# Order of the epilogues, pace of the sparse sums and the last chunks of a PEER block

## The chip, the cores and the metric

One Trainium2 chip, of which the kernel uses one core. The metric is the device time of one execution in microseconds; the median of three runs is given. The profile is of one further execution.

## What is computed

A transformer-like block on 512 tokens of width 1024: a mixer (gated convolution and a linear recurrence), then a PEER layer, which picks 16 of 16384 single-neuron experts for each of 8 heads and each token, and a final RMS norm. The part that the change touches is the last lines of this:

```
def peer block(xb):                      # 128 tokens
    idx = the 16 best experts of each of 8 heads; g = softmax of their scores
    act = gelu(einsum('phkd,pd->phk', expert_u[idx], xb))
    coef = g * act
    return einsum('phk,phkd->pd', coef, expert_v[idx])

x = x + g2[:, None, :] * peer(h, ...)
return rmsnorm(x, final_g)               # x * rsqrt(mean(x*x) + EPS) * final_g
```

## The kernel before

The four tiles of 128 tokens are treated in two ways. **Tile 0 is sparse**: for each of its 128 (head, pick) pairs GpSimd (POOL) gathers 128 rows of `expert_u` (512 KB, L802), DVE multiplies them with the tokens and adds up each row (`dots`, L823), and later the same with rows of `expert_v`: DVE adds the gathered rows, times their coefficient, to `ys` (`sums`, L837 and L839). The dots of 64 tokens of tile 1 are made in this way too. **Tiles 1 to 3 are dense**: all 16384 experts are evaluated, in 128 chunks of 128 experts, first with `u` (U stage, `u_chunk`), then with `v` (V stage). Matrix products are made exact enough by splitting an operand in a high and a low part and doing three products (high x high, high x low, low x high).

In the V stage, chunk n's 128 x 1024 block of `expert_v` is loaded on SP's queue into one of 4 `wraw` buffers (L70), ACT rounds it to `whi` (L75), DVE subtracts to get `wlo` (L80); each has 4 buffers. For every second chunk the gated coefficients of two chunks are made: `cf` (ACT L952, DVE L954), `ch` (ACT L958) and `cl` (DVE L965). PE then does 18 products of 512 columns for a chunk: 3 for each of 3 tiles and 2 halves, into six PSUM accumulators `acc` that stay open over all 128 chunks (`v_chunk`, L1070). The last VT = 3 chunks are held back and multiplied tile by tile (`v_half`, L1061 to L1063), so that tile 1's accumulators close before those of tiles 2 and 3.

Order: from the U stage to the end of the loop over chunks the program order of each engine is the order in which the code is written (`manual_schedule`, L1001 to L1116). Each chunk's turn in the loop (L1087) issues the load for the chunk five ahead, the rounding for three ahead, the subtraction for two ahead, the coefficients, PE's products, and then some steps of the sparse generator (dots, then sums). How many is a pace: `share` (L1111) grows linearly with n over NE - VE - QV chunks, less 0.31 for each chunk after RB = 32. Gathers run up to 6 steps ahead of the sums, in 5 `rows` buffers and 2 of `rows2`.

Behind the loop stand the loads of three rows into `gt` (the gate g2, its bias, the final gain; L1081), their sum (L1083), the loads of the residual `x1d` into `wraw` buffers (L1124), and `final(t)` for tiles 1, 2, 3 and 0: multiply by the gate row, add the residual, square and add up on ACT (L1134), 1/sqrt with one Newton step (`rsqrt_small`, L106), scale, store. From L1116 on a scheduler of the language decides the order of each engine, and it interleaves the four epilogues.

Of the kernel before, what the change touches and what calls it, by code (L numbers as in the profile page):

```python
# [8 lines left out]
F32 = mybir.dt.float32  # L9
# [4 lines left out]
AF = mybir.ActivationFunctionType  # L14
OP = mybir.AluOpType
# [3 lines left out]
D = 1024  # L19
KB = 8  # L20
NT = 4
NE = 128
EPS = 1e-6
# [11 lines left out]
def block_kernel(ctx, tc, xT, small, w_ada1, w_ada, b_ada, w_in, w_r, w_i, w_out, w_q, keys, uT, u, v, final_g, out):  # L35
    nc = tc.nc
# [69 lines left out]
    def rsqrt_small(dst, src, scale, n, seed=False):  # L106
        m = const.tile([128, 64], F32, name="rs_m")[:, :n]
        t = const.tile([128, 64], F32, name="rs_t")[:, :n]
        nc.vector.tensor_scalar(m, src, scale, EPS, op0=OP.mult, op1=OP.add)
        if seed:  # L110
            nc.scalar.activation(dst, m, AF.Abs_reciprocal_sqrt)
        else:
            nc.scalar.activation(t, m, AF.Sqrt)
            nc.vector.reciprocal(dst, t)
        nc.vector.tensor_mul(t, dst, dst)
        nc.vector.tensor_mul(t, t, m)
        nc.vector.tensor_scalar(t, t, -0.5, 1.5, op0=OP.mult, op1=OP.add)
        nc.vector.tensor_mul(dst, dst, t)
# [144 lines left out]
    g2d = dram.tile([2, 512], F32, name="g2d")  # L263
# [75 lines left out]
    for cb in range(4):  # L339
# [20 lines left out]
        r = mt("r")  # L360
# [24 lines left out]
        y = mix.tile([128, T], F32, name="y", bufs=2)  # L385
# [13 lines left out]
        y = mix.tile([128, T], F32, name="y", bufs=2)  # L399
# [19 lines left out]
    x1d = dram.tile([T, D], F32, name="x1d")  # L419
# [122 lines left out]
    rowp = ctx.enter_context(tc.tile_pool(name="rowp", bufs=1))  # L542
# [243 lines left out]
    rows = {}  # L786
# [69 lines left out]
    def w_load(k):  # L856
        if k < len(jobs):
            kind, i = jobs[k]
            wraw[k] = load_w(uT[i] if kind == "u" else
                             v[vorder[i] * 128:(vorder[i] + 1) * 128, :].rearrange("p (k e) -> p k e", k=KB))  # L860

    def w_high(k):
        if k < len(jobs):
            whi[k] = high(wraw[k])

    def w_low(k):
        if k < len(jobs):
            wlo[k] = low(wraw.pop(k), whi[k])
# [21 lines left out]
    def u_chunk(k, pool):  # L890
        c = jobs[k][1]
        if c:
            ps = pool.tile([128, NU], F32, name="ps_act", bufs=2)
            mm3(ps, whi.pop(k), wlo.pop(k), hd, ld, range(KB), True, True)
            u_evict()
            unread.append((c, ps))
        q = c // 2 - RB // 2 + 2
        if c % 2 == 0 and 0 <= q < v0 // 2:
            spill(q)
        pe[0] += 3530  # L900
        dve[0] += 1140
        ac[0] += 1400
# [21 lines left out]
    def v_gates(n):  # L924
        if n >= NE or n in gdone:
            return
        gdone.add(n)
        cc = vorder[n]
        if n < 16 and n % 8 == 0:
            gt = gt8[:, n // 8]  # L930
            for t in (2, 3, 1):
                nc.sync.dma_start(gt[:, 8 * t - 8:8 * t], Gd[t][:, :, cc:cc + 8, :].rearrange("g j i t -> j g i t"))
            for k in range(0, 8, 2):
                gbuf[n + k] = gt[:, :, k:k + 2, :]
        for t in range(1, NT):
            m = n + (4 - t if n < 16 else 13 - 3 * t)
            if m >= 16 and m % 16 == 0 and m < NE:
                load_g16(m, t)

    def v_act(q):  # L940
        if q < NE // 2:
            c = vorder[2 * q] // 2
            if act[c] is None:
                act[c] = ring.tile([128, 2, NU], F32, name="act", bufs=RB // 2)
                nc.sync.dma_start(act[c].rearrange("p c t -> p (c t)"), Ad[c])
# [15 lines left out]
    def v_rest(q):  # L961
        if q < NE // 2:
            cf, ch = coef[q]
            cl = vp.tile([128, 2, ND], FR, name="cl", bufs=2)
            nc.vector.tensor_sub(cl, cf, ch.bitcast(F32))  # L965
            coef[q] = (ch, cl)
# [34 lines left out]
    manual = ExitStack()  # L1001
    manual.enter_context(tc.manual_schedule())
    for k in range(CE):
# [12 lines left out]
        while dve[0] < RHO * pe[0] or k == KD:  # L1016
# [7 lines left out]
            n = next(gens[g], 0)  # L1024
# [13 lines left out]
        if k == KD:  # L1038
            ep.close()
            vp = ctx.enter_context(tc.tile_pool(name="vp", bufs=2, reuse_waits="tile"))  # L1040
            gp = ctx.enter_context(tc.tile_pool(name="gp", bufs=1, reuse_waits="tile"))
            late[:] = [gp, taken[0] + 10]
            gt8 = vp.tile([128, 2, NG, 8, 16], F32, name="gt", bufs=1)
        m = k - CE + XE
# [12 lines left out]
    def v_half(n, b, e):  # L1057
        hi, lo, ch, cl = vsp[n]
        es = slice(e * 512, (e + 1) * 512)
        bs = slice(b * 128, (b + 1) * 128)  # L1060
        nc.tensor.matmul(accs[b][e], ch[:, bs], hi[:, es], start=n == 0, stop=False)  # L1061
        nc.tensor.matmul(accs[b][e], ch[:, bs], lo[:, es], start=False, stop=False)
        nc.tensor.matmul(accs[b][e], cl[:, bs], hi[:, es], start=False, stop=n == NE - 1)  # L1063

    def v_chunk(n, b):
        hi, lo, ch, cl = vsp[n]
        bs = slice(b * 128, (b + 1) * 128)
        for st, mv, first, last in ((ch, hi, n == 0, False), (ch, lo, False, False), (cl, hi, False, n == NE - 1)):
            for e in range(2):
                nc.tensor.matmul(accs[b][e], st[:, bs], mv[:, e * 512:(e + 1) * 512], start=first, stop=last)  # L1070
# [4 lines left out]
    bro = lambda ap, n: bass.AP(tensor=ap.tensor, offset=ap.offset, ap=[[0, 128], [1, n]])  # L1075
    frow = []

    def final_rows():
        gt = fin[:, 0]
        for i, src in enumerate((bro(g2d, D), bro(b_ada[:, 5 * D:], D), bro(final_g, D))):  # L1080
            nc.sync.dma_start(gt[:, i, :], src)  # L1081
            frow.append(gt[:, i, :])
        nc.vector.tensor_add(frow[0], frow[0], frow[1])  # L1083

    sparse = chain(dot_gen, sum_gen)
    steps, done = len(usteps) - len(bdone) + 128, 0
    for k in range(CE, len(jobs)):  # L1087
        w_load(k + 5)
        w_high(k + 3)
        w_low(k + 2)  # L1090
        kind, n = jobs[k]
        if kind == "u":
            u_chunk(k, psP)
        else:
            q, e = divmod(n, 2)
            v_gates(n + 5)
            if e == 0:
                v_act(q + 4)
                v_gated(q + 1)
            else:  # L1100
                v_rest(q + 1)
            vsp[n] = [w.pop(k).rearrange("p k e -> p (k e)") for w in (whi, wlo)] + [c[:, e] for c in coef[q]]
            if n < NE - VT:
                for b in range(3):
                    v_chunk(n, b)
                del vsp[n]
            u_evict()
            pe[0] += 4090
            dve[0] += 2005
        if kind == "v":  # L1110
            share = min(max(n + 1 - QV, 0) / (NE - VE - QV), 1) * (steps + 0.31 * (NE - RB)) - 0.31 * max(n + 1 - RB, 0)  # L1111
            while done < share and next(sparse, None):
                done += 1
    fin = vp.tile([128, 2, 3, D], F32, name="gt", bufs=1)
    final_rows()
    manual.close()  # L1116
    g2r, _, fgr = frow
    yt = fin[:, 1]


    x1s = {}
    for t in (1, 2, 3, 0):
        x1s[t] = wring.tile([128, KB, 128], F32, name="wraw", bufs=WR).rearrange("p k e -> p (k e)")
        nc.sync.dma_start(x1s[t], x1d[t * 128:(t + 1) * 128, :])  # L1124

    def final(t):
        x1 = x1s[t]
        y = ys if t == 0 else yt[:, t - 1, :]
        ss = gp.tile([128, 2], F32, name="ss", bufs=2)
        for e in range(2):  # L1130
            es = slice(e * 512, (e + 1) * 512)
            nc.vector.tensor_mul(y[:, es], y[:, es] if t == 0 else accs[t - 1][e], g2r[:, es])
            nc.vector.tensor_add(y[:, es], y[:, es], x1[:, es])
            nc.scalar.activation(x1[:, es], y[:, es], AF.Square, accum_out=ss[:, e:e + 1])  # L1134
        nc.vector.tensor_add(ss[:, 0:1], ss[:, 0:1], ss[:, 1:2])
        rs = gp.tile([128, 1], F32, name="rs", bufs=2)
        rsqrt_small(rs, ss[:, 0:1], 1.0 / D, 1)
        for e in range(2):
            es = slice(e * 512, (e + 1) * 512)
            nc.vector.scalar_tensor_tensor(y[:, es], y[:, es], rs, fgr[:, es], op0=OP.mult, op1=OP.mult)  # L1140
            nc.sync.dma_start(out[t * 128:(t + 1) * 128, es], y[:, es])

    for b in range(3):
        for e in range(2):
            for n in range(NE - VT, NE):
                v_half(n, b, e)
            next(sparse, None)
        next(sparse, None)
        final(b + 1)
    for _ in sparse:  # L1150
        pass
    final(0)


XB = 64
# [3 lines left out]
AD = 500  # L1159
LEAD = 3500  # L1160
RHO = 1.0
VE = 1
KG = 4
HEAD = 6000
NS = 56000
# [3 lines left out]
GB_E = 5  # L1169
# [7 lines left out]
WR = 4  # L1177
SCB = 8
HQ = 4
VT = 3  # L1180


# [45 lines left out]
```

## Time and profile before

| | us |
|---|---|
| median of 3 runs | 1395.11 |
| lowest, highest | 1394.68, 1396.73 |
| the profiled execution | 1394.83 |
| its span (first to last instruction) | 1393.0 |
| PE's first product of the V stage | 817.3 |
| PE's last product ends | 1378.6 |

The mean granted clock of TensorE is 0.985. DMA queues moved 440.06 MB. The page's slices show DMA engines busy for nine tenths or more from the middle of the span on, and so are PE and DVE; the reading of these stretches is in the prediction. Names in the rows: `acc<-whi,ch` is what is written and what is read; L numbers are lines of the kernel before. An idle time in brackets names the engine's own idle time ahead of the row and what ended it.

### The profile page before, as it was taken

The numbers are of one execution on the slowest core, as the hardware profiler recorded it, in microseconds if no ns is written. First come the engines' busy times: TensorE is split into PE (matmuls) and PEld (weight loads), VectorE is DVE, ScalarE is ACT, GpSimd is POOL, SyncE is SP. The second block draws the span as 40 slices with busy tenths as digits, with TensorE's granted clock in tenths as the row PEclk, the third lists the DMA queues.
The fourth block names the chain that finished last, engine by engine and source line by source line (L and its number), as shares of the span: only waits on it lengthen the run. The fifth ranks groups of instructions, "written<-read, shape, count | busy, mean of one in ns | idle before, by whom it ended". The sixth has DMA issues, their size and how long they took to land.

```text
span 1393.0 us, 21402 instructions
## 1 busy us (share of the span) xinstructions
PE 1321.6 (95%) x7571; PEld 1135.5 (82%) x7571; DVE 1235.1 (89%) x2313; ACT 706.6 (51%) x1202; POOL 532.7 (38%) x334
## 2 busy tenths in 40 slices
PE   5999999989999999999999999899999999999995
PEld 2676787789989899998999998787878787878884
DVE  6878756999999999999999748799999889898998
ACT  4666644434567797787744443333243334333442
POOL 0000000000233244445445305576766566676760
PEclk9999999999999999999999999999999999999998
DMA  8776322224688899999999988999999999999994
GB/s 349 264 271 219 115 91 84 69 92 133 230 287 292 289 369 394 331 377 361 417 381 395 411 274 278 391 392 416 413 415 413 398 404 413 411 415 412 418 380 171
DMA packets 146928, 440.06 MB, mean 316 GB/s; under 512 B 14722, under 2 KB 42370, under 8 KB 144772
## 3 DMA queue, kind: packets, MB, share of 16 engines
q1 hardware_dynamic: 99812, 267.75, 52.2%
q0 software_dynamic: 46720, 169.89, 31.0%
q8 instruction: 59, 0.97, 0.3%
q10 hardware_dynamic: 288, 1.05, 0.2%
q14 instruction: 49, 0.40, 0.1%
HBM read 393.54 MB, written 45.09 MB: 315 GB/s over the span
## 4 chain that ended last, share of the span: by engine, by line
PE 47%; DVE 22%; DMA 13%; issue 12%; ACT 5%; DVEq 0%; SPq 0%; POOL 0%; ACTq 0%
DMA wraw<-in_v_dram 10%; PE acc L1070 8%; PE ps_act L89 6%; PE ps_act L91 6%; PE ps_act L90 6%; PE ps_z L89 5%; PE ps_z L90 5%; PE ps_z L91 5%; DVE wlo L80 4%; DVE scr L823 4%; DVE ys L839 3%; DMA Gd<-stg 2%; DVE cl L965 2%; DVE cf L954 2%; PE ps_gt L693 2%
## 5 line engine op out<-in xcount | busy, mean ns | idle before, releaser
L75 ACT ACTIVATE whi<-wraw 128x1024 fp32r<-128x1024 f32 x292 | 308.7, 1057 | 361.2 <-DMA wraw<-in_v_dram 204.6
L80 DVE TENSOR_TENSOR wlo<-wraw,whi 128x1024 fp32r<-128x1024 f32 x292 | 356.2, 1220 | 91.5 <-ACT whi L75 90.3
L89 PE MATMUL ps_act<-h,whi 128*128 128x320 f32 x1016 | 321.2, 316 | 5.4 <-ACT act L888 5.2
L91 PE MATMUL ps_act<-h,wlo 128*128 128x320 f32 x1016 | 316.2, 311 | 4.0 <-DVE wlo L80 4.0
L90 PE MATMUL ps_act<-h,whi 128*128 128x320 f32 x1016 | 315.9, 311 | 0.0
L802 POOL DMA_INDIRECT rows<-in_u_dram,idx_s x128 | 200.0, 1562 | 187.1 <-DVE scr L823 159.9
L802 POOL DMA_INDIRECT rows<-in_v_dram,idx_s x128 | 218.6, 1708 | 112.2 <-DVE ys L839 89.1
L1070 PE MATMUL acc<-whi,cl 128*128 128x512 f32 x750 | 233.5, 393 | 9.0 <-DVE cl L965 8.9
L1070 PE MATMUL acc<-whi,ch 128*128 128x512 f32 x750 | 232.8, 392 | 6.6 <-ACT ch L958 6.0
L1070 PE MATMUL acc<-wlo,ch 128*128 128x512 f32 x750 | 232.0, 390 | 0.0
L802 POOL DMA_INDIRECT rows<-in_u_dram,idx_b x64 | 108.9, 1702 | 264.4 <-DVE scr L823 171.6
L89 PEld LDWEIGHTS ps_act<-h,whi 128*128 128x128 f32 x1016 | 192.9, 190 | 8.0 <-ACT act L888 7.1
L91 PEld LDWEIGHTS ps_act<-h,wlo 128*128 128x128 f32 x1016 | 192.6, 190 | 4.3 <-DVE wlo L80 4.3
L90 PEld LDWEIGHTS ps_act<-h,whi 128*128 128x128 f32 x1016 | 192.8, 190 | 0.2
L1070 PEld LDWEIGHTS acc<-whi,cl 128*128 128x128 f32 x750 | 140.2, 188 | 43.5 <-DVE cl L965 15.1
L1070 PEld LDWEIGHTS acc<-whi,ch 128*128 128x128 f32 x750 | 140.7, 189 | 37.9 <-ACT ch L958 8.3
L1070 PEld LDWEIGHTS acc<-wlo,ch 128*128 128x128 f32 x750 | 141.4, 188 | 29.8
L839 DVE SCALAR_TENSOR_TENSOR ys<-rows,acts,ys 128x1024 f32<-128x1024 f32 x127 | 162.6, 1281 | 1.7
L823 DVE SCALAR_TENSOR_TENSOR scr<-rows,h2n 128x1024 f16<-128x1024 f32 x128 | 156.2, 1220 | 2.7 <-DMA rows<-in_u_dram,idx_s 1.0
L678 ACT ACTIVATE igh<-oh,gl 128x128 f16<-128x128 f16 x320 | 104.0, 431 | 47.3 <-DVE oh L662 47.1
L433 POOL DMA_DIRECT2D x1d<-xn x8 | 4.5, 570 | 258.8 <-ACT xn L432 258.8
L888 ACT ACTIVATE act<-ps_act 128x320 f32<-128x320 f32 x127 | 54.9, 433 | 90.6 <-PE ps_act L91 90.4
(277 smaller groups left out, 1750.6 us busy)
## 6 DMA issues: line engine op xcount, KB each, us to landing
wraw<-in_uT_dram SPq DMA_DIRECT2D x128, 512.0 KB, 6.4
wraw<-in_v_dram SPq DMA_DIRECT2D x128, 512.0 KB, 10.2
Gd<-stg SPq DMA_DIRECT2D x46, 512.0 KB, 8.9
wada<-in_w_ada_dram SPq DMA_DIRECT2D x16, 1024.0 KB, 5.3
Ad<-act SPq DMA_DIRECT2D x48, 320.0 KB, 7.0
act<-Ad SPq DMA_DIRECT2D x48, 320.0 KB, 12.6
h<-Gd SPq DMA_DIRECT2D x12, 1024.0 KB, 17.3
wraw<-in_w_in_dram SPq DMA_DIRECT2D x20, 512.0 KB, 6.0
```

Source lines behind the costliest of these rows:

```text
L75: nc.scalar.activation(hi, raw, AF.Copy)
L80: nc.vector.tensor_sub(lo, raw, hi.bitcast(F32))
L89: nc.tensor.matmul(ps, hi[:, k, :], xh(k), start=first and k == ks[0], stop=False)
L90: nc.tensor.matmul(ps, hi[:, k, :], xl(k), start=False, stop=False)
L91: nc.tensor.matmul(ps, lo[:, k, :], xh(k), start=False, stop=last and k == ks[-1])
L678: nc.scalar.activation(ig[:, 1, k // 2, :, k % 2], of[:, k // 2, 0, :, k % 2], AF.Copy, scale=gl[:, t0 + k:t0 + k + 1])
L693: nc.tensor.matmul(pg[:, k, :], oh[:, a, 1, :, b], ig[:, w, a, :, b], start=w == 0, stop=w == 1)
L802: nc.gpsimd.indirect_dma_start(out=r[:, :], out_offset=None, in_=table, in_offset=bass.IndirectOffsetOnAxis(ap=idxs[:, k:k + 1], axis=0))
L823: nc.vector.scalar_tensor_tensor(scr, rows.pop(n), 1.0, hn, op0=OP.mult, op1=OP.mult, accum_out=dst[:, k:k + 1])
L839: nc.vector.scalar_tensor_tensor(ys, rows.pop(k), acts[:, k:k + 1], ys, op0=OP.mult, op1=OP.add)
L888: nc.scalar.activation(act[c // 2][:, c % 2], ps, AF.Gelu)
L1070: nc.tensor.matmul(accs[b][e], st[:, bs], mv[:, e * 512:(e + 1) * 512], start=first, stop=last)
```

## The change

Five edits, all in the V stage and behind it:

1. VE goes from 1 to 5: the pace of the sparse steps reaches its end at chunk 122 instead of 126.
2. VT goes from 3 to 4, and the held-back chunks of tile 1 are multiplied chunk by chunk (both halves of one chunk, then the next); tiles 2 and 3 half by half, as before.
3. The three rows are loaded inside the loop, at chunk 119 (FL = 9), and tile 0's residual at chunk 120, into a `rows` buffer in place of a `wraw` buffer.
4. `manual_schedule` now covers the epilogues too, which are written as: row sum, `final(0)`, then for each tile PE's held-back chunks and `final(1)`, `final(2)`, `final(3)`.
5. Inside `final`, the mean's factor goes into ACT's square, the sum, EPS and 1/sqrt take one DVE and one ACT operation (`Abs_reciprocal_sqrt`), and the Newton step three small DVE operations.

```diff
@@ -1075,12 +1075,17 @@
     bro = lambda ap, n: bass.AP(tensor=ap.tensor, offset=ap.offset, ap=[[0, 128], [1, n]])
     frow = []
 
-    def final_rows():
-        gt = fin[:, 0]
-        for i, src in enumerate((bro(g2d, D), bro(b_ada[:, 5 * D:], D), bro(final_g, D))):
-            nc.sync.dma_start(gt[:, i, :], src)
-            frow.append(gt[:, i, :])
-        nc.vector.tensor_add(frow[0], frow[0], frow[1])
+    fin, x1s = [], {}
+
+    def final_load(n):
+        if n == NE - FL:
+            fin.append(vp.tile([128, 2, 3, D], F32, name="gt", bufs=1))
+            for i, src in enumerate((bro(g2d, D), bro(b_ada[:, 5 * D:], D), bro(final_g, D))):
+                nc.sync.dma_start(fin[0][:, 0, i, :], src)
+                frow.append(fin[0][:, 0, i, :])
+        if n == NE - FL + 1:
+            x1s[0] = rowp.tile([128, D], F32, name="rows", bufs=GB_E)
+            nc.sync.dma_start(x1s[0], x1d[0:128, :])
 
     sparse = chain(dot_gen, sum_gen)
     steps, done = len(usteps) - len(bdone) + 128, 0
@@ -1107,19 +1112,18 @@
             u_evict()
             pe[0] += 4090
             dve[0] += 2005
+            final_load(n)
         if kind == "v":
             share = min(max(n + 1 - QV, 0) / (NE - VE - QV), 1) * (steps + 0.31 * (NE - RB)) - 0.31 * max(n + 1 - RB, 0)
             while done < share and next(sparse, None):
                 done += 1
-    fin = vp.tile([128, 2, 3, D], F32, name="gt", bufs=1)
-    final_rows()
-    manual.close()
+    for _ in sparse:
+        pass
+    nc.vector.tensor_add(frow[0], frow[0], frow[1])
     g2r, _, fgr = frow
-    yt = fin[:, 1]
-
-
-    x1s = {}
-    for t in (1, 2, 3, 0):
+    yt = fin[0][:, 1]
+
+    for t in (1, 2, 3):
         x1s[t] = wring.tile([128, KB, 128], F32, name="wraw", bufs=WR).rearrange("p k e -> p (k e)")
         nc.sync.dma_start(x1s[t], x1d[t * 128:(t + 1) * 128, :])
 
@@ -1131,25 +1135,25 @@
             es = slice(e * 512, (e + 1) * 512)
             nc.vector.tensor_mul(y[:, es], y[:, es] if t == 0 else accs[t - 1][e], g2r[:, es])
             nc.vector.tensor_add(y[:, es], y[:, es], x1[:, es])
-            nc.scalar.activation(x1[:, es], y[:, es], AF.Square, accum_out=ss[:, e:e + 1])
-        nc.vector.tensor_add(ss[:, 0:1], ss[:, 0:1], ss[:, 1:2])
-        rs = gp.tile([128, 1], F32, name="rs", bufs=2)
-        rsqrt_small(rs, ss[:, 0:1], 1.0 / D, 1)
+            nc.scalar.activation(x1[:, es], y[:, es], AF.Square, scale=D ** -0.5, accum_out=ss[:, e:e + 1])
+        m, r, w = (gp.tile([128, 1], F32, name=nm, bufs=2) for nm in ("fm", "fr", "fw"))
+        nc.vector.tensor_scalar(m, ss[:, 0:1], ss[:, 1:2], EPS, op0=OP.add, op1=OP.add)
+        nc.scalar.activation(r, m, AF.Abs_reciprocal_sqrt)
+        nc.vector.tensor_scalar(w, m, r, r, op0=OP.mult, op1=OP.mult)
+        nc.vector.tensor_scalar(w, w, -0.5, 1.5, op0=OP.mult, op1=OP.add)
+        nc.vector.tensor_mul(r, r, w)
         for e in range(2):
             es = slice(e * 512, (e + 1) * 512)
-            nc.vector.scalar_tensor_tensor(y[:, es], y[:, es], rs, fgr[:, es], op0=OP.mult, op1=OP.mult)
+            nc.vector.scalar_tensor_tensor(y[:, es], y[:, es], r, fgr[:, es], op0=OP.mult, op1=OP.mult)
             nc.sync.dma_start(out[t * 128:(t + 1) * 128, es], y[:, es])
 
+    final(0)
     for b in range(3):
-        for e in range(2):
-            for n in range(NE - VT, NE):
-                v_half(n, b, e)
-            next(sparse, None)
-        next(sparse, None)
+        ne = [(n, e) for n in range(NE - VT, NE) for e in range(2)]
+        for n, e in ne if b == 0 else sorted(ne, key=lambda p: p[1]):
+            v_half(n, b, e)
         final(b + 1)
-    for _ in sparse:
-        pass
-    final(0)
+    manual.close()
 
 
 XB = 64
@@ -1159,7 +1163,8 @@
 AD = 500
 LEAD = 3500
 RHO = 1.0
-VE = 1
+VE = 5
+FL = 9
 KG = 4
 HEAD = 6000
 NS = 56000
@@ -1177,7 +1182,7 @@
 WR = 4
 SCB = 8
 HQ = 4
-VT = 3
+VT = 4
 
 
 # ---- launch: one core; inputs laid out as the kernel reads them ----
```

What this moves in the program order is shown at three places; the names are tiles, a number behind a name tells buffers apart.

DVE around the end of the sparse sums (L839). Before, the last `wlo` and `cl` (L80, L965, of chunks 126 and 127) have sums ahead of them and behind them:

```order
L80 TENSOR_TENSOR wlo<-wraw,whi 128x1024
L954 TENSOR_TENSOR cf<-act,h_9723 128x2x320
L839 SCALAR_TENSOR_TENSOR ys<-rows_13615,acts,ys 128x1024
L839 SCALAR_TENSOR_TENSOR ys<-rows,acts,ys 128x1024
L80 TENSOR_TENSOR wlo<-wraw,whi 128x1024
L965 TENSOR_TENSOR cl<-cf,ch 128x768
L839 SCALAR_TENSOR_TENSOR ys<-rows,acts,ys 128x1024
L839 SCALAR_TENSOR_TENSOR ys<-rows_13677,acts,ys 128x1024
L1083 TENSOR_TENSOR gt<-gt 128x1024
```

In the changed kernel the last sum is the one ahead of chunk 124's L80, and four `wlo` follow without one:

```order
L80 TENSOR_TENSOR wlo<-wraw,whi 128x1024
L965 TENSOR_TENSOR cl<-cf,ch 128x768
L839 SCALAR_TENSOR_TENSOR ys<-rows_13543,acts,ys 128x1024
L80 TENSOR_TENSOR wlo<-wraw,whi 128x1024
L954 TENSOR_TENSOR cf<-act,h_9723 128x2x320
L80 TENSOR_TENSOR wlo<-wraw,whi 128x1024
L965 TENSOR_TENSOR cl<-cf,ch 128x768
L80 TENSOR_TENSOR wlo<-wraw,whi 128x1024
L954 TENSOR_TENSOR cf<-act,h_9723 128x2x320
L80 TENSOR_TENSOR wlo<-wraw,whi 128x1024
L965 TENSOR_TENSOR cl<-cf,ch 128x768
L1122 TENSOR_TENSOR gt<-gt 128x1024
```

All sums have moved ahead of the last four weight subtractions.

DVE in the epilogues. Before, a stretch of it (acc_9323 is tile 2's second half, acc_9324 and acc_9325 tile 3's, `ys` tile 0):

```order
L1135 TENSOR_TENSOR ss<-ss 128x1
L1133 TENSOR_TENSOR gt<-gt,wraw 128x512
L109 TENSOR_SCALAR rs_m<-ss 128x1
L1132 TENSOR_TENSOR gt<-acc_9323,gt 128x512
L1133 TENSOR_TENSOR ys<-ys,wraw 128x512
L1133 TENSOR_TENSOR gt<-gt,wraw 128x512
L1132 TENSOR_TENSOR gt<-acc_9324,gt 128x512
L114 RECIPROCAL rs<-rs_t 128x1
L1133 TENSOR_TENSOR gt<-gt,wraw 128x512
L115 TENSOR_TENSOR rs_t<-rs 128x1
```

In the changed kernel one tile's epilogue, that of tile 1, with the first row of the next:

```order
L1136 TENSOR_TENSOR gt<-acc_9320,gt 128x512
L1137 TENSOR_TENSOR gt<-gt,wraw 128x512
L1136 TENSOR_TENSOR gt<-acc_9321,gt 128x512
L1137 TENSOR_TENSOR gt<-gt,wraw 128x512
L1140 TENSOR_SCALAR fm<-ss 128x1
L1142 TENSOR_SCALAR fw<-fm,fr 128x1
L1143 TENSOR_SCALAR fw<-fw 128x1
L1144 TENSOR_TENSOR fr<-fr,fw 128x1
L1147 SCALAR_TENSOR_TENSOR gt<-gt,fr 128x512 x2
L1136 TENSOR_TENSOR gt<-acc_9322,gt 128x512
```

Operations of several tiles that stood between each other now stand tile after tile.

SP's queue behind the last load of spilled activations (`act`). Before:

```order
L70 DMA wraw<-in_v_dram 128x1024 x4
L1081 DMA gt<-g2d 128x1024
L1081 DMA gt<-in_b_ada_dram 128x1024
L1081 DMA gt<-in_final_g_dram 128x1024
L1124 DMA wraw<-x1d 128x1024 x4
```

In the changed kernel:

```order
L70 DMA wraw<-in_v_dram 128x1024
L1084 DMA gt<-g2d 128x1024
L1084 DMA gt<-in_b_ada_dram 128x1024
L1084 DMA gt<-in_final_g_dram 128x1024
L70 DMA wraw<-in_v_dram 128x1024
L1088 DMA rows<-x1d 128x1024
L70 DMA wraw<-in_v_dram 128x1024 x2
L1128 DMA wraw<-x1d 128x1024 x3
```

The three row loads have moved ahead of the last three weight loads, tile 0's residual ahead of the last two.

## Prediction

> **What bounds the kernel now.** I read the page's engine totals first, then the table by time windows, then who waits for whom, then the timeline of a few stretches. The totals say little: PE and DVE are both busy nearly everywhere.
>
> ```profile
> PE 1321.6 (95%) x7571; PEld 1135.5 (82%) x7571; DVE 1235.1 (89%) x2313; ACT 706.6 (51%) x1202; POOL 532.7 (38%) x334
> ```
>
> The dense V stage runs from 817 us to the end. The windows give busy time and count for PE, weight loads, DVE, ACT and POOL, then granted clock, DMA share and GB/s; the wait table gives total, times and longest.
>
> ```profile
> 1150.00:1200.00 50.00, 48.23 (x212) 39.32 (x211) 49.72 (x47) 20.74 (x27) 34.81 (x21) 1.00 1.03 412
> 1300.00:1350.00 50.00, 50.00 (x223) 41.40 (x222) 49.72 (x47) 20.28 (x26) 34.79 (x20) 1.00 1.02 403
> ACT whi L75 <- DMA wraw<-in_v_dram: 203.6, 72, 10.7
> DVE wlo L80 <- ACT whi L75: 34.9, 14, 5.7
> PE acc L1070 <- DVE cl L965: 8.9, 12, 2.3
> ```
>
> In both windows DVE is idle for 0.28 us of 50. From 840 to 1365 us it waits 34.9 us in 14 places, always for a weight chunk that a burst of loads made late; between those it issues without a pause. PE waits for DVE in 12 places. So DVE sets the pace after each burst, and PE catches up in between. The last such place is at chunk 108:
>
> ```profile
> 1289.80 1.22 DVE L80 TENSOR_TENSOR wlo<-wraw,whi 128x1024 fp32r<-128x1024 f32 x1
> 1291.67 2.60 DVE L839 SCALAR_TENSOR_TENSOR ys<-rows,acts,ys 128x1024 f32<-128x1024 f32 x2
> 1294.19 1.22 DVE L80 TENSOR_TENSOR wlo<-wraw,whi 128x1024 fp32r<-128x1024 f32 x1
> 1295.32 0.95 DVE L965 TENSOR_TENSOR cl<-cf,ch 128x768 fp32r<-128x768 f32 x1
> 1296.33 0.73 PE L1070 MATMUL acc<-whi,cl 128*128 128x512 f32 x2 [0.35 <-DVE cl L965]
> 1360.82 0.61 PE L1070 MATMUL acc<-whi,ch 128*128 128x512 f32 x2
> 1364.90 0.39 PE L1061 MATMUL acc<-whi,ch 128*128 128x512 f32 x1
> 1378.25 0.39 PE L1063 MATMUL acc<-whi,cl 128*128 128x512 f32 x1
> ```
>
> PE resumes at 1296.33 when DVE's cl arrives. From there it does not wait until after 1364.90, a chunk every 4.08 us (1360.82 to 1364.90). It ends at 1378.6, but the program ends on DVE:
>
> ```profile
> 1360.72 1.22 DVE L80 TENSOR_TENSOR wlo<-wraw,whi 128x1024 fp32r<-128x1024 f32 x1
> 1361.85 0.81 DVE L954 TENSOR_TENSOR cf<-act,h 128x640 f32<-128x640 f32 x1
> 1361.02 1.06 ACT L75 ACTIVATE whi<-wraw 128x1024 fp32r<-128x1024 f32 x1 [3.02 <-PE acc L1070]
> 1366.24 0.95 DVE L965 TENSOR_TENSOR cl<-cf,ch 128x768 fp32r<-128x768 f32 x1
> 1367.11 2.60 DVE L839 SCALAR_TENSOR_TENSOR ys<-rows,acts,ys 128x1024 f32<-128x1024 f32 x2
> 1369.62 1.22 DVE L1083 TENSOR_TENSOR gt<-gt 128x1024 f32<-128x1024 f32 x1
> 1370.94 0.69 DVE L1132 TENSOR_TENSOR gt<-acc,gt 128x512 f32<-128x512 f32 x1
> 1388.33 1.42 DVE L1140 SCALAR_TENSOR_TENSOR ys<-ys,rs,gt 128x512 f32<-128x512 f32 x2
> ```
>
> DVE's epilogue work starts at 1369.62 and its last instruction ends at 1389.75, 20.1 us later. The last store and the close take the other 3.25 us of the span of 1393.0.
>
> **Term 1: the sparse steps move forward.** The pace formula of the V loop spreads the sparse steps over NE - VE - QV chunks, which goes from 124 to 120. How many there are shows in the counts of L823 (two records each) and L839 by window:
>
> ```profile
> 817.00:1107.00 290.00, 98.28 (x160) 0.99 0.97 380
> 817.00:1107.00 290.00, 30.07 (x24) 0.99 0.97 380
> 1107.00:1295.00 188.00, 92.87 (x73) 1.00 1.03 410
> 1295.00:1370.00 75.00, 39.70 (x31) 1.00 0.98 386
> ```
>
> That is 80 dots, and 128 sums with the one at L837: 208 steps. With the formula's 0.31 x 96, 237.8 are spread; at chunk n the changed kernel is (n - 2) x 237.8 x (1/120 - 1/124) = 0.064 (n - 2) steps ahead, so at chunk 108 about 7 more steps lie in front of the cl for which PE waits. A step costs DVE 1.26 us (two sums from 1291.67 to 1294.19). 7 x 1.26 = **8.8 us**. Each step also brings a 512 KB gather, at 403 to 412 GB/s again about 1.3 us of transfer.
>
> Does DVE's idle time swallow this? It arises when loads are late, and weight loads, gate loads and gathers are all released by DVE's progress (a slot is free when DVE has read it). One more step per 16 chunks gives the DMAs 1.26 us more time and 1.3 us more work, so I expect the idle time to stay. Then PE gets past chunk 108 later by 8.8 us and cannot recover: it already runs without waits behind it, and its chunk 124 starts at 1360.82 + 8.8 = 1369.6. The bounds are 0 (all swallowed) and 8.8; I take 8.8.
>
> **Term 2: where the epilogue can start.** After chunk 123 no sparse sum is left, so the 2.5 us of sums at 1367.11 no longer stand between cl and the row sum (L1083, now L1122). What is late next is the last whi: at 1361.02 it waited for PE's end of chunk 123 (a buffer of 4). Then L80 at 1362.1, 1.13 us to the next (1360.72 to 1361.85), cl at 1363.2, 0.87 us to the next (1366.24 to 1367.11): the row sum starts at 1364.1 in before's time, with term 1 at **1372.9**, against 1369.62. That it cannot be much earlier follows from DVE alone: the same lows, coefficients and sums stand ahead of it as before.
>
> **Term 3: the epilogues in written order.** These rows give the pieces:
>
> ```profile
> 1371.55 0.68 DVE L1132 TENSOR_TENSOR ys<-ys,gt 128x512 f32<-128x512 f32 x1
> 1372.15 0.68 DVE L1133 TENSOR_TENSOR gt<-gt,wraw 128x512 f32<-128x512 f32 x1
> 1372.87 0.63 ACT L1134 ACTIVATE wraw<-gt 128x512 f32<-128x512 f32 x1 [9.26 <-DVE gt L1133]
> 1373.40 0.19 ACT L1134 ACTIVATION_READ_ACCUMULATOR wraw<-gt 128x1 f32 x1
> 1377.28 1.28 ACT L113 ACT_TABLE_LOAD   x1
> 1378.57 0.20 ACT L113 ACTIVATE rs_t<-rs_m 128x1 f32<-128x1 f32 x1
> 1383.36 0.15 DVE L117 TENSOR_SCALAR rs_t<-rs_t 128x1 f32<-128x1 f32 x1
> 1383.43 0.14 DVE L109 TENSOR_SCALAR rs_m<-ss 128x1 f32<-128x1 f32 x1
> 1383.49 0.15 DVE L1135 TENSOR_TENSOR ss<-ss 128x1 f32<-128x1 f32 x1
> 1387.56 0.16 DVE L115 TENSOR_TENSOR rs_t<-rs 128x1 f32<-128x1 f32 x1
> 1387.75 0.16 DVE L116 TENSOR_TENSOR rs_t<-rs_t,rs_m 128x1 f32<-128x1 f32 x1
> ```
>
> Independent 512-wide operations stand 0.60 us apart (1371.55 to 1372.15); one that reads the result before it about 0.10 later than its duration (1369.62 + 1.22, next at 1370.94), so 0.78. The four multiplies and adds of a tile: 0.78 + 0.60 + 0.78, then 0.72 until ACT's square starts (1372.15 to 1372.87), 0.72 until its sum is read out (1373.59). The sum on DVE 0.2, the handoff and the reciprocal root on ACT 0.3, three dependent small operations at 0.19 (1387.56 to 1387.75) 0.6, the two scalings 1.35. That is 6.0 us a tile, of which DVE stands idle about 1.9, where before it filled such waits with another tile. The removed three small operations of each tile are within this. Tile 0's chain has the table load too, after its second square: 1.28 less 0.2 that it covers, 1.1. Sum: 1.3 for the row sum, 7.1, then 6.0 x 3 = **26.4 us** against 20.1. 0.02 off each of ten operations a tile makes it 25.6; so 25.5 to 27.
>
> The Trainium skill bears on this in "VectorE: DVE Perf Modes", section "The DRAIN you can't avoid": chained operations with a semaphore after each took as long as without, so only the count matters. Here the rows differ for small operations: independent ones are 0.06 to 0.07 us apart (1383.36, 1383.43, 1383.49), dependent ones 0.19. By that rule the tail would be about 0.5 us a tile, 2 us in all, shorter. The page "ScalarE: Activation LUTs", section "What ACT_TABLE_LOAD costs", adds a drain of 1.38 us to a switch; the row shows 1.28 in all, the next ACT instruction starting right behind it, and with the drain tile 0 would end 1.4 us later.
>
> **Costed at nothing.** PE does the same 72 matmuls for its last four chunks; by tile it wants chunks 126 and 127 some 1.4 us sooner, and gets cl just in time; should it wait 1 us, it ends near 1387 at the latest, and tile 3's epilogue comes after that anyway. The row loads and tile 0's rows move ahead of weight loads 125 and 126 to 127 on SP's queue, 2 MB or 5 us at 403 GB/s. The whi at 1361.02 had waited 3.02 us for PE with its data there, so about 3 us are covered; what is queued behind the row buffer's wait on SP are those two weight loads, and PE waits for them. Bounds 0 and 3 us; I take 0. No gather is left to be issued behind the buffer that tile 0's rows take, so POOL loses nothing.
>
> **Sum.** Last DVE instruction at 1372.9 + 26.4 = 1399.3 against 1389.75: 9.5 us later (of these 6.3 from the longer tail, 3.3 from the later start). The profiled execution took 1394.83 us, 0.28 below the median: 1394.83 + 9.5 = **1404.3 us**.
>
> **Rivals.** (a) DVE's idle time swallows the extra steps, not slower than before: the point is whether the 34.9 us shrink by at least 6. If all 8.8 go, the row sum starts at 1364.1, the end is at 1390.5, the time 1395.6: no change. For it: loads are late only now and then, and the change asks DVE to reach each burst later. Against it: the argument of term 1, and DVE's 0.28 us idle in the two windows. Chance 0.13. (b) As (a), and dependent operations or handoffs cost less than in before's rows, 0.9 to 1.2 us a tile: a tail of 21.6 to 22.8 us, 1390.8 to 1392.0, faster. For it: the skill's rule; against it: the spacing of 0.19. Chance 0.09. (c) The sums arrive as I say, but the idle time shrinks by half of 8.8: 1399.9. Chance 0.2, within the forecast's side. (d) The loads moved forward delay the last weights by their bound of 3 us, or larger bursts do: 1407.3. Chance 0.13. (e) The forecast: 0.45.
>
> **How the numbers follow.** A measurement of this kernel tells 0.2%, 2.8 us, from no change. (c), (d) and (e) are slower by more than that: 0.78; (a) is the same, 0.13; (b) faster, 0.09. The range leaves out (b) and the lowest of (a), and the far end of (d): 1395.5 to 1407.5.
>
> **What would show it.** In the changed profile: PE's start of chunk 124 near 1369 to 1370 (term 1; near 1361 for (a)); DVE's wait for whi still near 35 us up to there; the row sum L1122 near 1373; tiles' first multiplies L1136 6 us apart with DVE idle at L1140, L1142 and L1147; PE finished some 12 us before DVE. Wrong would be the forecast if that wait shrinks by 6 us or more, or a tile's epilogue takes under 5 us.

## The result and the profile after

The changed kernel is slower by 0.8%: 1407.4 us median of 6 runs (1404.61 to 1408.86), against 1395.92 of 6 runs of the kernel before beside it (1394.68 to 1400.57). The ratio is 1.0078, 95% interval 1.0064 to 1.0093. The prediction was 1404.3 us, range 1395.5 to 1407.5: the median lies 0.1 us inside its far end, the profiled execution (1408.13 us) 0.6 us beyond it. Three executions of the experiments below ran in a slow state (one of e4 at 1862.51 us, two of e8 at 4582.7 and 7382.44) and are left out of the ratios.

Rows picked from the timeline of the changed kernel around its end, with the first product of the V stage as first row (columns as in the prediction's timeline rows):

```profile
819.36 0.74 PE L1070 MATMUL acc<-whi,ch 128*128 128x512 f32 x2 [0.53 <-ACT act L888]
...
1373.05 0.39 PE L1061 MATMUL acc<-whi,ch 128*128 128x512 f32 x1
1373.25 1.06 ACT L75 ACTIVATE whi<-wraw 128x1024 fp32r<-128x1024 f32 x1 [3.02 <-PE acc L1070]
1374.34 1.23 DVE L80 TENSOR_TENSOR wlo<-wraw,whi 128x1024 fp32r<-128x1024 f32 x1 [2.12 <-ACT whi L75]
1376.35 1.22 DVE L1122 TENSOR_TENSOR gt<-gt 128x1024 f32<-128x1024 f32 x1
...
1381.15 0.21 DVE L1140 TENSOR_SCALAR fm<-ss 128x1 f32<-128x1 f32 x1 [0.79 <-ACT rows L1138]
1382.66 0.27 DVE L1142 TENSOR_SCALAR fw<-fm,fr 128x1 f32<-128x1 f32 x1 [1.30 <-ACT fr L1141]
1384.68 0.68 DVE L1136 TENSOR_TENSOR gt<-acc,gt 128x512 f32<-128x512 f32 x1
1388.22 0.21 DVE L1140 TENSOR_SCALAR fm<-ss 128x1 f32<-128x1 f32 x1 [0.79 <-ACT wraw L1138]
1388.70 0.27 DVE L1142 TENSOR_SCALAR fw<-fm,fr 128x1 f32<-128x1 f32 x1 [0.27 <-ACT fr L1141]
1389.55 0.39 PE L1063 MATMUL acc<-whi,cl 128*128 128x512 f32 x1
1390.72 0.68 DVE L1136 TENSOR_TENSOR gt<-acc,gt 128x512 f32<-128x512 f32 x1
1396.75 0.69 DVE L1136 TENSOR_TENSOR gt<-acc,gt 128x512 f32<-128x512 f32 x1
1401.45 1.42 DVE L1147 SCALAR_TENSOR_TENSOR gt<-gt,fr 128x512 f32<-128x512 f32 x2
```

Chunk 124 starts at 1373.05, where before it was at 1360.82. The row sum starts at 1376.35 and DVE's last instruction ends at 1402.87: a tail of 26.5 us. Tiles 1 to 3 begin 6.03 us apart, and in each DVE stands idle at L1140 and L1142. PE has been done for 13 us when DVE ends.

That the tail grew mostly by idle time is one line of the windows, first of the kernel before, then of the changed one (window, then its length and busy time and count of PE, PEld, DVE, ACT, POOL):

```profile
1369.60:1389.80 20.20, 9.04 (x40) 7.14 (x39) 19.59 (x54) 7.44 (x21) 0.00 (x0) 0.82 0.20 79
```

```profile
1376.35:1402.90 26.55, 13.48 (x59) 10.81 (x58) 20.52 (x42) 7.88 (x21) 0.00 (x0) 0.84 0.15 60
```

DVE is busy for 19.59 of 20.20 us before and 20.52 of 26.55 after, with 42 operations in place of 54 (the short norm): 0.9 us more busy time, and 6.0 us idle instead of 0.6.

The other half is the V stage. Busy time and count of L839 from PE's first product to its start of chunk 108, before and after:

```profile
817.00:1294.80 477.80, 122.94 (x96) 0.99 1.00 392
```

```profile
819.40:1307.80 488.40, 132.07 (x104) 0.99 1.00 392
```

Eight more sums (104 - 96) are done before chunk 108, which starts 11 us later, counted from the stage's first product (1307.8 - 819.4 against 1294.8 - 817.3). Pieces of the chain that ended last in the changed kernel (start, us, what):

```profile
1281.54 12.01 DMA wraw<-in_v_dram
...
1294.37 1.21 DVE ys L839
...
1298.94 74.28 PE acc L1070 x320
...
1376.44 1.15 DVE gt L1122
```

A weight load is the long piece up to 1293.5; from 1298.94 PE runs without a wait, in the end at 4.08 us a chunk, and then DVE ends it. What an extra step costs in front of that, the chain alone does not say; the experiments with sums and gathers left out do.

### The profile page after: what moved, and what is told of

Same layout as the page of the kernel before. It is cut to its first block, busy times and chain, and to the rows that moved or that the text cites. A ratio compares the mean times of both kernels' runs of the same rounds, so it can differ in the third digit from the quotient of the medians.

```text
span 1406.4 us, 21393 instructions
## 1 busy us (share of the span) xinstructions
PE 1325.4 (94%) x7571; PEld 1137.1 (81%) x7571; DVE 1237.2 (88%) x2301; ACT 707.1 (50%) x1202; POOL 535.3 (38%) x334
## 3 DMA queue, kind: packets, MB, share of 16 engines
q10 hardware_dynamic: 288, 1.05, 0.2%
## 4 chain that ended last, share of the span: by engine, by line
PE 32%; DVE 25%; DMA 19%; issue 17%; ACT 5%; POOL 1%; SPq 0%; DVEq 0%; ACTq 0%; POOLq 0%
DMA wraw<-in_v_dram 14%; PE acc L1070 5%; DVE wlo L80 5%; DVE scr L823 5%; PE ps_z L89 5%; PE ps_z L90 5%; PE ps_z L91 5%; PE ps_act L89 3%; PE ps_act L91 3%; PE ps_act L90 3%; DMA rows<-in_u_dram,idx_s 2%; DVE ys L839 2%; ACT whi L75 2%; DVE cf L954 2%; DMA wraw<-in_uT_dram 2%
## 5 line engine op out<-in xcount | busy, mean ns | idle before, releaser
L80 DVE TENSOR_TENSOR wlo<-wraw,whi 128x1024 fp32r<-128x1024 f32 x292 | 356.4, 1220 | 96.6 <-ACT whi L75 95.5
L839 DVE SCALAR_TENSOR_TENSOR ys<-rows,acts,ys 128x1024 f32<-128x1024 f32 x127 | 162.7, 1281 | 1.8
```

The costliest lines, as they stand in the source:

```text
L80: nc.vector.tensor_sub(lo, raw, hi.bitcast(F32))
L839: nc.vector.scalar_tensor_tensor(ys, rows.pop(k), acts[:, k:k + 1], ys, op0=OP.mult, op1=OP.add)
```

## The experiments

Times are medians; ratios are to the kernel before on the same chip, with their 95% intervals.

| label | kernel | us | ratio |
|---|---|---|---|
| (the change) | | 1407.4 | 1.0078 (1.0064 to 1.0093) |
| e1_pace_back | change, VE = 1 | 1404.18 | 1.0053 (1.0033 to 1.0072) |
| e2_scheduler_tail | change, epilogues by the scheduler | 1398.75 | 1.0022 (1.0006 to 1.0038) |
| e3_pace_alone | before, VE = 5 | 1403.7 | 1.0051 (1.0033 to 1.0068) |
| e4_pace_later | before, VE = -3 | 1395.1 | 0.9988 (0.9976 to 0.9999) |
| e5_ops_out | change, 8 of DVE's sums left out | 1408.26 | 1.0089 (1.0067 to 1.0111) |
| e6_gathers_out | change, 8 gathers left out | 1400.0 | 1.0031 (1.0017 to 1.0045) |
| e7_short_norm | before, short norm | 1396.73 | 1.0006 (0.9991 to 1.0021) |
| e8_pool_tile0 | e7, row sum and tile 0's work on GpSimd | 1396.09 | 1.0004 (0.9987 to 1.0022) |
| e9_pool_keep_sum | e8, row sum on DVE | 1396.51 | 0.9999 (0.9987 to 1.0011) |
| e10_before_gathers_out | before, 8 gathers left out | 1388.6 | 0.9951 (0.9935 to 0.9967) |
| e11_before_ops_out | before, 8 of DVE's sums left out | 1396.23 | 1.0 (0.9987 to 1.0013) |
| e12_late_pace_pool | e9, VE = -3 | 1395.41 | 0.9994 (0.9982 to 1.0007) |

### The two large parts, undone one at a time

e1: the pace goes back, and tile 0's residual is loaded behind the loop, since the sums still need the `rows` buffers.

```diff
-VE = 5
+VE = 1
-        if n == NE - FL + 1:
-            x1s[0] = rowp.tile([128, D], F32, name="rows", bufs=GB_E)
-            nc.sync.dma_start(x1s[0], x1d[0:128, :])
...
-    for t in (1, 2, 3):
+    for t in (0, 1, 2, 3):
```

> The changed kernel with the pace set back (VE 1) and tile 0's residual loaded behind the loop into a wraw buffer; written order, by-tile chunks, early row loads and short norm stay. Theory (V stage held up by DVE's extra steps, and a longer tail by the written order): DVE's row sum starts at about 1369.6 us as before, the tail from there stays at 26.5 us, 1402 us in all, 6 above before. Rival 1 (all of the loss is in the V stage): 1396. Rival 2 (the loss comes from the moved loads and the by-tile chunks): near 1407.

The timeline's ends of the tail:

```profile
1373.43 1.22 DVE L1119 TENSOR_TENSOR gt<-gt 128x1024 f32<-128x1024 f32 x1
...
1398.52 1.42 DVE L1144 SCALAR_TENSOR_TENSOR gt<-gt,fr 128x512 f32<-128x512 f32 x2
```

The tail is 26.5 us again (1398.52 + 1.42 - 1373.43), as long as with the change's pace. The median came down by 0.25% of 1396, 3.5 us, where about five were expected; the two intervals overlap, so this gain alone is not clear of noise. The row sum stands at 1373.43, not near 1369.6 as expected. Part of that is a weight chunk that came late:

```profile
1358.90 1.06 ACT L75 ACTIVATE whi<-wraw 128x1024 fp32r<-128x1024 f32 x1 [6.76 <-DMA wraw<-in_v_dram]
```

DVE then waits 1.44 us for this `whi`. With VE = 1 and the row loads at their old place (before, e7) ACT waits for PE there and not for data, so the moved loads are the likely reason; no run takes them back alone. The rest is no larger than what profiles of one pace differ by: in e7, too, the row sum stands at 1373.43.

e2: the scheduler orders the epilogues again; pace, early loads, four chunks by tile and short norm stay.

```diff
+    manual.close()
     nc.vector.tensor_add(frow[0], frow[0], frow[1])
...
         final(b + 1)
-    manual.close()
```

> The changed kernel with only the epilogues given back to the scheduler, which interleaves them. Theory: the V stage stays as late as in the changed kernel (chunk 124 near 1371 to 1373), the tail from the row sum shrinks from 26.5 us to between 19.5 and 23 (PE ends some 13 us behind the row sum, so the last tile may wait for it): 1400.5 to 1404. Rival 1 (all of the loss is in the V stage): 1407, no change.

```profile
1373.19 1.22 DVE L1122 TENSOR_TENSOR gt<-gt 128x1024 f32<-128x1024 f32 x1
...
1391.04 1.42 DVE L1148 SCALAR_TENSOR_TENSOR gt<-gt,fr 128x512 f32<-128x512 f32 x2
```

Its window from the row sum on:

```profile
1373.20:1392.50 19.30, 13.35 (x59) 10.62 (x57) 18.54 (x42) 7.55 (x21) 0.00 (x0) 0.93 0.21 82
```

The tail is 19.3 us, 7.2 less than with the written order and the same 42 operations of DVE: 0.8 us idle instead of 6.0, and 2.0 us less busy. The time comes down by 0.56%, 7.8 us, more than expected and clear of noise. The two undone singly give 3.5 + 7.8 = 11.3 us; the whole change costs 0.78%, 10.9 us.

### The pace alone, both ways

e3 and e4 are the kernel before with nothing but the number changed:

```diff
-VE = 1
+VE = 5    (e3)
+VE = -3   (e4)
```

> The kernel before with nothing but VE 5. Theory: 7 more sums ahead of chunk 108, chunk 124 starts 8.8 to 10 us later than before, DVE's row sum 3.3 to 5 us later, the interleaved tail then waits for PE's last products: 4 to 9 us slower than before, 1400 to 1405. Rival (DVE's idle time takes the steps): no change, chunk 124 at 1361 and DVE's wait for whi smaller by 8.

> The kernel before with VE -3: the sparse steps are spread over 4 chunks more, 6 fewer sums ahead of chunk 108, about ten left behind the loop. Theory (DVE's total work to the end is what counts): PE's chunk 124 starts up to 7.5 us earlier, but DVE ends no earlier: within 2 us of before, 1394 to 1398. Rival (PE's chain sets the end): 6 to 8 us faster, 1388 to 1390.

e3, the kernel before with VE = 5, costs 0.51%, 7.1 us, as expected. Its timeline has chunk 124 13.5 us and the row sum 8.0 us later than before, more than the 10 and 5 expected at most, and DVE now waits for PE in the epilogues:

```profile
1374.33 0.61 PE L1070 MATMUL acc<-whi,ch 128*128 128x512 f32 x2
...
1377.63 1.22 DVE L1083 TENSOR_TENSOR gt<-gt 128x1024 f32<-128x1024 f32 x1
...
1384.72 0.69 DVE L1132 TENSOR_TENSOR gt<-acc,gt 128x512 f32<-128x512 f32 x1 [0.62 <-PE acc L1063]
...
1386.77 0.69 DVE L1132 TENSOR_TENSOR gt<-acc,gt 128x512 f32<-128x512 f32 x1 [0.56 <-PE acc L1063]
```

So the pace alone costs more here than e1 gave back, and, by the medians, more than e2, which has the same pace and costs 0.22% (the two intervals just overlap). From chunk 124's start to DVE's end it is 26.0 us in e3 and 22.6 us in e2: some of the change's other parts (chunks by tile, early loads, short norm) give something back. Which of them does was not separated, and so it stays open which of the two large parts is the dearer one.

e4, with VE = -3, moves steps the other way:

```profile
1353.01 0.62 PE L1070 MATMUL acc<-whi,ch 128*128 128x512 f32 x2
...
1357.21 6.56 DVE L839 SCALAR_TENSOR_TENSOR ys<-rows,acts,ys 128x1024 f32<-128x1024 f32 x5
1363.69 1.22 DVE L1083 TENSOR_TENSOR gt<-gt 128x1024 f32<-128x1024 f32 x1
...
1387.61 1.41 DVE L1140 SCALAR_TENSOR_TENSOR ys<-ys,rs,gt 128x512 f32<-128x512 f32 x2
```

PE reaches chunk 124 7.8 us earlier, but DVE ends at 1389.02, 0.7 earlier than before's 1389.75: the sums now stand behind the last weight chunk, and the 0.12% it gains (its interval ends just short of 1) is less than what I called measurable. That PE's chain sets the end of the kernel before is refuted.

### Which resource a sparse step costs

A step is a 512 KB gather and a DVE instruction, 1.3 us of either by the prediction. e5 takes the instruction out of 8 of the 128 sums of the changed kernel, e6 the gather; e11 and e10 do the same to the kernel before.

```diff
-            if k == 0:
+            if k % 16 == 15:
+                rows.pop(k)
+            elif k == 0:
```

```diff
-                gath(v, idx_s, kk, kk)
+                if kk % 16 != 15:
+                    gath(v, idx_s, kk, kk)
+            if k % 16 == 14:
+                rows[k + 1] = rows[k]
```

> The changed kernel without DVE's operation of every 16th sparse sum (8 of 128 left out of tile 0's result), all gathers kept. Six of them stand ahead of chunk 108. Theory (DVE sets the pace of the V stage): chunk 108 starts 6 x 1.26 = 7.6 us earlier than in the changed kernel, 1399 to 1400 in all. Rival (the gathers' transfers set it): no change, near 1407, DVE's wait for whi larger by 7.

> The changed kernel without the gather of every 16th sparse sum, whose DVE operation adds the row block before once more (tile 0's result differs by that); 8 gathers of 512 KB are left out, 6 ahead of chunk 108. Theory: DVE still issues every operation, so at most DVE's wait for whi shrinks a little: 0 to 3 us faster than the changed kernel. Rival: 7 to 8 us faster, 1399 to 1400, and DVE's wait for whi falls by as much.

> The kernel before without DVE's operation of every 16th sparse sum (8 of 128), all gathers kept. If transfers set the pace of the V stage: chunk 124 where it was (1358 to 1363), DVE's wait for whi up from 33 to 40 us or more, and the end earlier only by what of it stands behind the last weight chunk, 1.3 us (the last sum is one of the eight): 1394 to 1396 us. If DVE sets the pace: chunk 124 some 8 us earlier and 1386 to 1389 us.

> The kernel before with the gather of every 16th sparse sum left out (8 of 128; the sum adds the block before it once more), DVE's work unchanged. If transfers set the V stage's pace in the kernel before too: 8 gathers at 1.3 us bring chunk 124 some 7 to 10 us forward and DVE's wait for whi down from 33 to about 25 us; the end comes forward by less, 4 to 8 us, since DVE has the same tail: 1388 to 1392 us. If DVE sets the pace (as the prediction had it): no change, 1395 to 1397, and chunk 124 at 1360 to 1363.

DVE's row of the table of waits between 855 and 1300 us (total, times, longest): of the kernel before, e11 and e10, then of the changed kernel, e5 and e6.

```profile
DVE wlo L80 <- ACT whi L75: 32.9, 13, 5.7
```

```profile
DVE wlo L80 <- ACT whi L75: 40.7, 18, 7.6
```

```profile
DVE wlo L80 <- ACT whi L75: 27.9, 15, 4.9
```

```profile
DVE wlo L80 <- ACT whi L75: 33.6, 14, 7.9
```

```profile
DVE wlo L80 <- ACT whi L75: 44.5, 18, 7.9
```

```profile
DVE wlo L80 <- ACT whi L75: 25.6, 14, 5.4
```

Without DVE's instructions neither kernel gets faster (1.0089 against 1.0078; 1.0 against 1): DVE waits 7.8 and 10.9 us more for its weights instead. Without the gathers both do, by 0.47 and 0.49%, 6.6 and 6.8 us, and DVE, with the same work as ever, waits 5.0 and 8.0 us less. So in the V stage a step is paid in transfers. The gather takes an instruction of GpSimd with it, but GpSimd's time is no likely price: it was busy for 292 of the 445 us from 855 to 1300 in the kernel before, and waited mostly for DVE to free a buffer. What I had expected of e5 and e6, that DVE sets the pace, fell; e10 and e11 came out as the transfers say, but for chunk 124: e11's is at 1364.38, 1.4 behind the stretch expected, and e10's at 1355.08 is 5.7 us forward, not 7 to 10.

How long PE took from its first product to chunk 124 sorts the profiles by their gathers:

| kernels | V stage up to chunk 124, us |
|---|---|
| VE = -3 (e4, e12) | 535.9, 537.0 |
| VE = 1, 8 gathers out (e10) | 538.6 |
| VE = 1 (before, e1, e7, e8, e9, e11) | 543.5, 545.1, 549.7, 544.2, 545.0, 545.9 |
| VE = 5, 8 gathers out (e6) | 544.6 |
| VE = 5 (change, e2, e3, e5) | 553.7, 551.4, 556.8, 557.2 |

Four chunks of pace are worth about 9 us here (means 536.4, 545.6, 554.8). Single profiles of one pace differ by about 6 us, so none of them alone tells a difference of that size.

### Attempts to beat both

e7 is the kernel before with the change's short norm (the hunk inside `final` of its diff, from `AF.Square` to the Newton step). e8 also gives the row sum and tile 0's two multiplies and two adds to GpSimd, idle by then; e9 leaves the row sum on DVE; e12 is e9 with VE = -3. The edit of e8 beside its `nc.gpsimd.tensor_add` for the row sum:

```diff
-            nc.vector.tensor_mul(y[:, es], y[:, es] if t == 0 else accs[t - 1][e], g2r[:, es])
-            nc.vector.tensor_add(y[:, es], y[:, es], x1[:, es])
+            eng = nc.gpsimd if t == 0 else nc.vector
+            eng.tensor_mul(y[:, es], y[:, es] if t == 0 else accs[t - 1][e], g2r[:, es])
+            eng.tensor_add(y[:, es], y[:, es], x1[:, es])
```

> The kernel before with nothing but the changed kernel's short norm (one DVE and one ACT operation for sum, EPS and 1/sqrt, three small DVE operations). Theory: three small operations of 0.07 us fewer a tile where they are independent, and two dependent ones of 0.19 fewer in the last tile's chain: 0.5 to 1.5 us faster than before. Rival (the chain is hidden behind other tiles throughout): no change.

> The kernel before with the short norm, the row sum and tile 0's two multiplies and two adds on GpSimd in place of DVE, the scheduler's order kept. Theory (what counts is DVE's work up to the end): 1.3 + 4 x 0.6 = 3.7 us of DVE work less behind the sums, 4 to 5 us faster than before with the norm: 1391 to 1393. Rival 1: the last tile's chain behind PE's end at 1378.6 holds the end at 1386 or later in the profile, 3 us faster at most. Rival 2: GpSimd needs over 3 us an operation, and tile 0 ends last: no gain or slower.

> The kernel before with the short norm and tile 0's two multiplies and two adds on GpSimd, the row sum back on DVE. If GpSimd's row sum beside DVE's cf was what spoiled the last experiment: L954 takes 0.8 us again, PE does not stall for cl at chunk 126, and DVE, rid of four operations at about 0.65 us, of which two or three beside GpSimd's take about 0.65 us more each, ends 1 to 2 us earlier than with the short norm alone: 1394 to 1395.5 us. If any GpSimd work here costs DVE as much as it frees: 1396 to 1397, as with the short norm alone.

> As the experiment with the short norm and tile 0's multiplies and adds on GpSimd, and VE -3: the sparse steps are moved back by four chunks. If a step moved is paid once either way, in transfers of the V stage or in DVE time behind it: chunk 124 near 1353, sums go on behind the last weight chunk, and the time is that of the same kernel with VE 1 within 2 us, 1393 to 1396. If PE's chain had set the end: some 5 us faster, 1389 to 1391.

None is measurably faster than before: all four intervals hold 1. The 4 to 5 us expected of e8 and the 1 to 2 us of e9 over e7 did not come; the 0.5 to 1.5 us expected of e7 lie within its interval and are neither shown nor refuted. In e8's timeline the row sum on GpSimd holds up DVE's coefficients, and PE waits 2.85 us for `cl` at the last chunks, where it waited 1.05 in the kernel before:

```profile
1360.65 3.00 POOL L1083 TENSOR_TENSOR gt<-gt 128x1024 f32<-128x1024 f32 x1 [5.30 <-DMA gt<-in_final_g_dram]
1361.30 3.03 DVE L954 TENSOR_TENSOR cf<-act,h 128x640 f32<-128x640 f32 x1
...
1368.91 0.80 PE L1063 MATMUL acc<-whi,cl 128*128 128x512 f32 x1 [2.85 <-DVE cl L965]
1369.50 0.63 PE L1061 MATMUL acc<-whi,ch 128*128 128x512 f32 x1
1369.93 0.63 PE L1062 MATMUL acc<-wlo,ch 128*128 128x512 f32 x1
```

L954 took 3.03 us where its other rows say 0.8. In e9 it is back at 0.82, and still nothing is gained; its timeline behind the row sum:

```profile
1374.27 1.22 DVE L1083 TENSOR_TENSOR gt<-gt 128x1024 f32<-128x1024 f32 x1
1375.58 3.06 POOL L1133 TENSOR_TENSOR ys<-ys,gt 128x512 f32<-128x512 f32 x2 [15.04 <-DVE gt L1083]
1375.59 1.29 DVE L1133 TENSOR_TENSOR gt<-acc,gt 128x512 f32<-128x512 f32 x2
1376.80 2.38 DVE L1134 TENSOR_TENSOR gt<-gt,wraw 128x512 f32<-128x512 f32 x2
...
1391.03 1.41 DVE L1144 SCALAR_TENSOR_TENSOR ys<-ys,fr,gt 128x512 f32<-128x512 f32 x2
```

Two multiplies from PSUM (`acc`) take their 1.29 us beside GpSimd; two adds, both operands in SBUF, take 2.38. From the row sum to the end it is 18.2 us, against 18.7 in e7's profile. The expected 1 to 2 us are not there; how much of them the slowed adds take, and how much the handoffs, I did not separate. e12 is at 1395.41 us, inside what was expected, and shows the exchange of e4 a second time: chunk 124 at 1356.26 (expected near 1353), and ten sums behind the last weight chunk's L80.

## Why the prediction came out as it did

The sum was 3.1 us short of the median. In the profiled execution, 1408.13 us, it was 3.8 short: the row sum 3.4 later than the 1372.9 said, the tail 0.1 longer, 0.3 more behind DVE's end.

**Term 3 was right, by its mechanism.** 26.5 us against 26.4, 6.03 a tile against 6.0. Window and e2 confirm what it rested on: the same operations, with waits that no other tile fills. DVE's idle time is 6.0 us over the four tiles, 1.5 a tile where the prediction said about 1.9. By the Trainium skill's rule on chained operations ("VectorE: DVE Perf Modes", "The DRAIN you can't avoid"), as the prediction worked it out, the tail would have been some 2 us shorter; it is not. Tile 0's table load kept DVE waiting 1.30 us, and ACT's next operation starts 0.02 us behind the load. The Trainium skill's "ScalarE: Activation LUTs", section "What ACT_TABLE_LOAD costs", adds a drain of about 1.38 us to the load; the trace does not show that drain.

**Term 2 was right.** The last whi waited 3.02 us for PE, as in before, and the row sum came 3.3 us after chunk 124's start (1376.35 - 1373.05), as in the prediction (1372.9 - 1369.6).

**Term 1 had the right size for the wrong reason.** The step that failed is "So DVE sets the pace after each burst, and PE catches up in between". e5 and e11 show it: DVE's time can be given back in the V stage and nothing comes of it. What sets the pace up to chunk 108 is the transfers, of which the prediction's own windows had the sign, a DMA share of 1.02 and 1.03 at 403 to 412 GB/s; it read the 0.28 us of DVE's idle time in 50 instead. That the size came out right was luck: a gather happens to take about as long as its sum (512 KB at some 410 GB/s, an estimate of 1.28 us, and 1.26), so the sum came out near: eight steps at 1.28 would be 10.2, and the stage up to chunk 124 took 553.7 us instead of 543.5, 10.2 more, against 8.8 said for seven steps. By the means of the table it is 9. The remaining 2.0 of the 3.4 us were there at chunk 8, before anything had moved (864.3 before, 866.3 after), and other profiles' stages begin as far apart: no effect of the change.

**The rivals.** (a) and (c), idle time that swallows the steps, did not hold: the wait stood at 33.6 us between 855 and 1300, 32.9 before. Over the prediction's stretch, 840 to 1365, it grew from 34.9 to 38.6. The reason given against them, that a step brings the DMAs as much work as time, is the part of that paragraph that held. (b) fell with the tail. (d), moved loads delaying the last weights, is not seen in the changed kernel: from 1316 us on ACT's whi waits for PE and never for data. In e1, with VE = 1, a late weight chunk is seen, so the 0 us holds for this pace only. The time of (d), 1407.3, is near the measured one, but for another reason.

**Costed at nothing.** PE by tile on four chunks had one weight load wait 0.53 us for cl and ended 13 us before DVE: that it does not set the end held.

## What to carry to other kernels

When several engines are nearly full, "who never pauses" does not say who sets the pace: take a small part of one resource's work away without touching the other's, both ways round, and see which the time follows. Work that is moved out of a stretch that DVE bounds is only a gain if the stretch that takes it has room in every resource that the work uses; here a step cost 1.3 us either way, and moving it four chunks in either direction never gained more than 0.12%. Chains of small dependent operations at a program's end should be left interleaved across tiles: written tile by tile, the same 42 operations took 26.5 us here, interleaved 19.3.

## What the runs showed of the hardware that was not expected

PE ran at half rate for a while after some stalls. In the changed kernel it stalled for 1.19 and 1.76 us just before 1299; two windows of it and one of e8, behind the stall of 2.85 us, the last three numbers being granted clock, DMA share and GB/s:

```profile
1294.00:1302.00 8.00, 5.04 (x15) 3.51 (x14) 7.93 (x8) 3.73 (x5) 5.20 (x3) 0.79 1.05 409
1302.00:1310.00 8.00, 8.00 (x36) 6.57 (x36) 7.96 (x8) 3.66 (x6) 5.33 (x4) 1.00 1.03 421
```

```profile
1368.90:1374.60 5.70, 5.69 (x13) 4.46 (x14) 4.38 (x4) 0.73 (x2) 3.09 (x3) 0.50 0.27 92
```

The granted clock is 0.79 in the first, 1.00 in the second and 0.50 in e8's, where products stood 0.43 us apart instead of 0.227 until 1374.6. Behind single stalls of 1.05 us (before, 1367.24) and 1.50 us (e9, 1371.89) it stayed at 1.00. In e8 the 5.7 us at half rate cost about 2.8 on top of the stall. The Trainium skill's "TensorE: Matmul & The Clock Gate", section "What's actually happening", says that the clock halves after an idle window of about 3.4 us and returns after a busy one; both places agree with a half rate that lasts some microseconds, but no stall here was as long as that window, so shorter stalls sufficed.

GpSimd and DVE block each other. The Trainium skill's "SBUF — State Buffer", section "SBUF: two separate sides", states that a DVE operation with two SBUF inputs and a GpSimd operation that reads SBUF exclude each other for the whole instruction. e8's rows agree: L954 began at 1361.30 and ended at 1364.33, 0.68 us after GpSimd's row sum (1360.65 + 3.00), a little under its own length of 0.8. So does e9's difference between multiplies from PSUM and adds from SBUF.
